# Expert biases as three float32r matmuls, and w_down's rows in contiguous groups, in a mixture-of-experts block

## The chip, the cores and the metric

The kernel runs on one core of a Trainium2 chip. The metric is the device time of one execution in microseconds (us). Names used here: PE is TensorE, PEld its weight loads, DVE VectorE, ACT ScalarE, POOL GpSimd, SP SyncE, which here does nothing but issue DMAs. L77 is line 77 of the kernel before.

## The reference

One layer of a diffusion backbone, for 256 latent tokens and 256 context tokens of 1024 numbers, all float32. A first half mixes tokens (a modulated norm, an input projection, a state-space scan and a gated delta net beside each other, an output projection, a residual). The second half, in which the change lies, is a mixture of 32 experts, of which each token uses 4:

```python
logits = t @ w_router + b_router
top_val, top_idx = lax.top_k(logits, 4)
weights = softmax(top_val)                      # -> combine[token, expert]
for e in range(32):
    gu = t @ w_gate_up[e] + b_gate_up[e]        # 1024 -> 2048
    gate, up = gu[:, :1024], gu[:, 1024:]
    gate = minimum(gate, 7.0); up = clip(up, -7.0, 7.0)
    act = (up + 1.0) * gate * sigmoid(gate * 1.702)
    out = out + combine[:, e:e+1] * (act @ w_down[e] + b_down[e])
x = rmsnorm(x + gt2 * out, norm_f)
```

## The kernel before

**Stages.** `front()` is the first half of the layer and ends with `merge()` (the output projection and the second norm); `moe()` is the router and the experts. All engines but SP get their order from a scheduler that goes by priorities in program order; SP's order is that in which the code issues its loads.

**An expert.** Its tokens are gathered into 64 slots (`gather`: products with one-hot matrices `oh`). Class `Expert` then computes in four steps. `gu(end)` multiplies the slots' columns `xT` (128 rows x 64 slots, stationary) by row chunks of w_gate_up, 128 rows of 2048 columns each; there are 8. The two halves of the array's columns work side by side: gate and up are tiles of 512 columns in PSUM, of which one half of 1024 hidden columns lies on partitions 0 to 63 and the other on 64 to 127. `swiglu` makes `ut` of them, `down` transposes `ut` to `aT` and multiplies by w_down in 4 pieces of 256 rows, `weigh` and `scatter` add the result to the tokens. In `moe()` the steps of two experts interleave:

```python
cur.gu(6); nxt = expert(e + 1); cur.gu(8); cur.swiglu()
nxt.gu(4); cur.down(); nxt.gu(5); cur.weigh(); cur.scatter()
```

**Weights.** An expert takes 12 tiles `w` of 1 MiB, 8 of w_gate_up and 4 of w_down: 384 in all, 8 matmul instructions each in the trace. `moe_stream` gives their order, `wload` issues them on SP's queue into a ring of 18 buffers (`WREG`), which the front's tensors leave in that order; 10 loads go ahead of the experts. Twelve buffers are of 8 KB per partition. The others (K, four of `ld`, `s1`) are two tiles of 4 KB, so that a weight tile comes in two DMAs of 512 KB, with runs of 4 KB per partition. A w_down tile puts rows 256f + p and 256f + 128 + p on partition p: two runs of 4 KB, in any buffer.

**Biases.** `bias` holds b_gate_up as 128 rows of 512 (four for each expert) and b_down as 64 rows. A product adds one row to all slots: its stationary matrix is a column of the identity, broadcast over 64 columns (`row`), its moving one `bias`. There are 4 such float32 products ahead of an expert's first w_gate_up chunk and 2 ahead of its first w_down chunk, 12 instructions in the trace, as `bias,ident`. Below b_down lie two rows of norm_f, which two products and two ACT copies spread over the partitions for the last expert.

## Time and profile before

| | |
|---|---|
| Time, 3 runs | 1507.41 us median, 1506.1 to 1511.52 |
| Span of the profiled execution | 1498.9 us |
| Front | 0 to some 501 us |
| Last output projection and routing | 501 to 532 us |
| Experts | 532 to 1484 us |
| End (scatter, last norm, output) | 1484 to 1498.9 us |

The profiled execution has no device time of its own beside the span; the runs' median is 8.5 us above it. The page gives busy times of the engines, the span in 40 slices, and what the DMA engines moved. A weight tile is 1.0486 MB, so bytes of the weights' queue and counted `w` matmuls can be set against each other stretch by stretch.

### The profile page before, as it was taken

Reading aid. Unit: us, or ns where it says so; the run is one execution under the profiler, and the core shown is the slowest. Engines: PE = TensorE matmul, PEld = TensorE weight load, DVE = VectorE, ACT = ScalarE, POOL = GpSimd, SP = SyncE. Lnnn points to the kernel's source line nnn. Section 1 sums busy time; section 2 is a strip of 40 time slices with the busy share of each in tenths; the row PEclk is TensorE's granted clock in tenths of the full one; section 3 lists DMA queues with packets and bytes.
Section 4 is the critical chain, followed back from the end, with each engine's and each line's share of the span. In section 5 each row is a group of like instructions: output and inputs, shape, how many; then the busy total and the mean of one; then the engine's idle time right before and its main releaser. Section 6 shows DMA issues by size and latency. Waiting matters only on the chain. (4 is left out here: it accounts for less than half of the span.)

```text
span 1498.9 us, 20035 instructions
## 1 busy us (share of the span) xinstructions
PE 1407.0 (94%) x8102; PEld 659.2 (44%) x8102; DVE 556.6 (37%) x1070; ACT 263.7 (18%) x578; POOL 203.2 (14%) x272
## 2 busy tenths in 40 slices
PE   5798796799989999999999999999999999999995
PEld 2275474687667543333333333333333333333331
DVE  3878788554424421232213212321321222123123
ACT  3434233233300111010101101110111111011111
POOL 1728499321100000000000000000000000000000
PEclk9699898799989999999999999999999999999997
DMA  9465355831185889999999999999999999999993
GB/s 309 133 192 118 130 166 145 134 93 43 48 266 185 307 320 368 415 415 413 414 414 415 413 415 415 414 415 412 415 414 416 415 411 416 413 416 411 413 414 147
DMA packets 157259, 473.22 MB, mean 316 GB/s; under 512 B 29090, under 2 KB 68175, under 8 KB 135081
## 3 DMA queue, kind: packets, MB, share of 16 engines
q1 hardware_dynamic: 137501, 460.06, 79.6%
q10 hardware_dynamic: 19276, 10.77, 3.3%
q0 software_dynamic: 384, 1.05, 0.6%
q8 instruction: 66, 1.08, 0.3%
q14 instruction: 32, 0.26, 0.0%
HBM read 467.68 MB, written 4.15 MB: 315 GB/s over the span
## 5 line engine op out<-in xcount | busy, mean ns | idle before, releaser
L77 PE MATMUL ps<-w,xT 128*64 128x512 f32 x2048 | 485.0, 598 | 0.1
L77 PEld LDWEIGHTS ps<-w,xT 128*64 128x64 f32 x2048 | 141.9, 137 | 279.9 <-issue 251.5
L77 PE MATMUL ps<-w,aT 128*64 128x512 f32 x1024 | 233.3, 599 | 0.7 <-ACT aT L83 0.7
L1701 DVE SCALAR_TENSOR_TENSOR od<-ps,cs,gt 128x512 f32<-128x512 f32 x32 | 24.0, 751 | 494.1 <-PE ps L77 494.1
L77 PEld LDWEIGHTS ps<-w,aT 128*64 128x64 f32 x1024 | 76.7, 138 | 146.9 <-issue 137.4
L80 POOL TENSOR_TENSOR frs<-frs,mhalf 128x1 f32<-128x1 f32 x2 | 1.1, 540 | 970.9 <-DVE frs L340 970.9
L77 PE MATMUL ps<-h,wsp 128*128 128x256 f32 (+1 forms) x672 | 113.2, 317 | 17.2 <-ACT gs L83 6.7
L80 DVE TENSOR_TENSOR x<-x,ps 128x512 f32<-128x512 f32 x128 | 85.2, 684 | 86.5 <-PE ps L77 86.5
L77 PEld LDWEIGHTS ps<-h,wsp 128*128 128x128 f32 x672 | 94.7, 202 | 35.5 <-issue 9.6
L77 PE MATMUL ps<-bias,ident 128*64 128x512 f32 (+2 forms) x388 | 101.4, 605 | 0.1
L83 ACT ACTIVATE odh<-od 128x512 fp32r<-128x512 f32 x31 | 19.5, 629 | 419.8 <-DVE od L1701 419.8
L80 DVE TENSOR_TENSOR wsp<-win,wsp 128x512 fp32r<-128x512 f32 x72 | 60.9, 852 | 41.0 <-ACT wsp L83 40.6
L77 PE MATMUL ps<-hh,wsp 128*128 128x512 f32 x192 | 55.9, 422 | 15.1 <-DVE wsp L80 13.4
L77 PE MATMUL ps<-h,oh 128*64 128x512 f32 x248 | 63.8, 602 | 0.0
L77 PE MATMUL ps<-wm,sc 128*32 128x512 f32 x192 | 48.5, 671 | 14.5 <-DMA wm<-in_w_mod_dram 14.5
L83 ACT ACTIVATE wsp<-win 128x512 fp32r<-128x512 f32 x72 | 43.7, 626 | 70.9 <-PE ps L77 28.1
L83 ACT ACTIVATE aT<-ps 128x512 f32<-128x512 f32 x32 | 19.1, 597 | 181.3 <-PE ps L1686 181.3
L77 PEld LDWEIGHTS ps<-bias,ident 128*64 128x64 f32 (+2 forms) x388 | 23.0, 134 | 62.4 <-issue 29.1
L83 ACT ACTIVATE sgm<-gt 128x512 f32<-128x512 f32 x32 | 20.1, 628 | 170.1 <-DVE gt L1673 170.1
L77 PEld LDWEIGHTS ps<-hh,wsp 128*128 128x128 f32 x192 | 36.1, 198 | 30.3 <-DVE wsp L80 15.4
L703 DVE SCALAR_TENSOR_TENSOR cacc<-raw,cols,cacc 128x512 f32<-128x512 f32 (+1 forms) x48 | 46.0, 959 | 5.9 <-ACT cacc L83 5.5
L1673 DVE TENSOR_SCALAR gt<-ps 128x512 f32<-128x512 f32 x32 | 22.1, 691 | 55.1 <-PE ps L77 55.1
(369 smaller groups left out, 1464.4 us busy)
## 6 DMA issues: line engine op xcount, KB each, us to landing
w<-in_w_gate_up_dram SPq DMA_DIRECT2D x172, 1024.0 KB
w<-in_w_gate_up_dram SPq DMA_DIRECT2D x168, 512.0 KB
w<-in_w_down_dram SPq DMA_DIRECT2D x84, 1024.0 KB
w<-in_w_down_dram SPq DMA_DIRECT2D x88, 512.0 KB
wm<-in_w_mod_dram SPq DMA_DIRECT2D x48, 512.0 KB
win<-in_w_in_dram SPq DMA_DIRECT2D x36, 512.0 KB
wo<-in_w_out_dram SPq DMA_DIRECT2D x8, 512.0 KB
wa<-in_w_branch_a_dram SPq DMA_DIRECT2D x4, 512.0 KB
```

The source lines that it names most:

```text
L77: self.nc.tensor.matmul(out, lhsT, rhs, start=start, stop=stop, **kw)
L80: (eng or self.nc.vector).tensor_tensor(out, a, b, op=op)
L83: self.nc.scalar.activation(out, in_, func, **kw)
L703: nc.vector.scalar_tensor_tensor(acc[:, rows], rt[:, rows, k:k + 64], sc, acc[:, rows], op0=OP.mult, op1=OP.add)
L1673: V.tensor_scalar(gt, pz[0], 7.0, None, op0=OP.min)
L1701: V.scalar_tensor_tensor(od, self.pd, self.cs, k.gt2, op0=OP.mult, op1=OP.mult)
```

## The change

- **Biases.** A product in float32r takes one pass, but does not keep all bits of a float32, so the biases are split into two parts that each fit and add up exactly. `bias` becomes three tiles of 128 rows: the upper parts of 64 bias rows on partitions 0 to 63, the remainders on 64 to 127. Each is loaded twice (`braw`, two DMAs of 128 KB on ACT's queue, in a buffer of `s5`), copied by ACT into float32r, and DVE subtracts the copy on the lower half. `dup` is a 64-column matrix with two ones in each column. For each expert two POOL copies (`pick`) broadcast its columns into stationary tiles `selsg` (for gate and up) and `selsd` (for down), one buffer each. Two products of 128x128 on 512 columns add the gate and up biases, one the down bias.
- **w_down.** Partition p of a half of w_down now gets four rows in sequence, 4p to 4p + 3; a tile takes two of them, one run of 8 KB. The transposes of `ut` read every fourth column to match.
- **The buffer K** is one tile of 8 KB per partition, so its weight tiles come in one DMA.
- **norm_f** is broadcast by a DMA on GpSimd's queue into the buffer R3, in place of two products and two copies.
- **Other buffers.** gt2 moves from tag g1 to rw; `mod2`'s bias row is loaded at its step (4, 1), in a buffer of `s5`. The overflow path, which runs only where an expert has more than 64 tokens, changes in the same way.

The diff, without comments and docstrings:

```diff
-    TAGS = dict(s1=(1024, 2), s5=(512, 4), p5=(512, 3), g1=(1024, 2), g5=(512, 3), c2=(256, 4), rw=(544, 2), cs=(4, 3))
-    REGS = ("H0", "H1", "R0", "R1", "R2", "R3", "U", "XC", "XL", "V", "Q", "PA", "PB", "GA")
+    TAGS = dict(s1=(1024, 2), s5=(512, 4), p5=(512, 3), g1=(1024, 2), g5=(512, 3), c2=(256, 4), rw=(544, 2), cs=(4, 3),
+                sg=(256, 1), sd=(128, 1))
+    REGS = ("H0", "H1", "R0", "R1", "R2", "R3", "U", "XC", "XL", "V", "Q", "PA", "PB", "GA", "K")
...
-    def rr(self, reg, name):
-        assert reg == "K"
-        return [self.wk.tile([128, 1024], F32, name=name, tag=f"r{reg}{i}", bufs=1) for i in range(2)]
...
+                    ps.append(self.pt("o"))
+                if (j, b) == ((0, 0) if nb == 1 else (4, 1)):
...
-                    ps.extend([self.pt("o"), bm])
-                p, bm = ps
+                    ps.append(bm)
+                p, bm = ps[0], ps[-1]
...
-        return self.mod_run(2048, 2, None)
+        return self.mod_run(2048, 2, "s5")
...
-        self.ct = self.rr("K", "ct")
+        self.ct = self.r("K", "ct").rearrange("p (a d) -> p a d", a=2)
...
-            nc.sync.dma_start(self.ct[a], dram(I["ctx"], 128 * D * a, [[D, 128], [1, D]]))
+            nc.sync.dma_start(self.ct[:, a], dram(I["ctx"], 128 * D * a, [[D, 128], [1, D]]))
...
-        src = [ct[0], ct[1], self.xt[:, 0], self.xt[:, 1]]
+        src = [ct[:, 0], ct[:, 1], self.xt[:, 0], self.xt[:, 1]]
...
-                self.kT = [t[:, x:x + 512] for t in self.rr("K", "kT") for x in (0, 512)]
+                k = self.r("K", "kT")
+                self.kT = [k[:, 512 * i:512 * i + 512] for i in range(4)]
...
-        dn = lambda e, f: dram(I["w_down"], (e * D + f * 256) * D, [[D, 128], [128 * D, 2], [1, D]])
+        dn = lambda e, f: dram(I["w_down"], (e * D + 512 * (f // 2) + 2 * (f % 2)) * D, [[4 * D, 128], [1, 2 * D]])
...
-        if rg == "K":
-            return self.rr(rg, "w")
...
-                    self.nc.sync.dma_start(w[0][:, f * D:f * D + D], src[:, f])
+                    self.nc.sync.dma_start(w[0][:, f * D:f * D + D], src[:, f * D:f * D + D])
...
-        bias = self.w([128, 2, 512], "bias", "g1")
-        for i, (nm, a, b) in enumerate((("b_gate_up", 0, 128), ("b_down", 0, 64), ("norm_f", 64, 66))):
-            nc.scalar.dma_start(bias[a:b, min(i, 1)], dram(I[nm], 0, [[512, b - a], [1, 512]]))
-        self.gt2 = self.w([128, 512], "gt2", "g1")
+        bt = [self.w([128, n], nm, "g1", F32R) for n, nm in ((1024, "bias"), (576, "biad"))]
+        bias = [bt[0][:, :512], bt[0][:, 512:], bt[1][:, :512]]
+        for i, (nm, r) in enumerate((("b_gate_up", 0), ("b_gate_up", 64), ("b_down", 0))):
+            t = self.w([128, 512], "braw", "s5")
+            for h in range(2):
+                nc.scalar.dma_start(t[64 * h:64 * h + 64], dram(I[nm], 512 * r, [[512, 64], [1, 512]]))
+            self.act(bias[i], t, AF.Copy)
+            self.tt(bias[i][64:], t[64:], bias[i][64:].bitcast(F32), OP.subtract)
+        dup = bt[1][:, 512:]
+        self.tt(dup, self.ident[:, :64], self.ident[:, 64:], OP.add)
+        self.gt2 = self.w([128, 512], "gt2", "rw")
...
-        row = lambda n, x: self.ident[:n, x:x + 1].to_broadcast([n, CAP])
+        def pick(x, n, tag):
+            v = self.w([128, n * CAP], "sel" + tag, tag, F32R)
+            nc.gpsimd.tensor_copy(v.rearrange("p (n s) -> p n s", s=CAP), dup[:, x:x + n, None].to_broadcast([128, n, CAP]))
+            return v
...
-                for h in range(2):
-                    p = self.pt("s")
-                    self.mm(p, self.ident[64:66, 64 + h:65 + h].to_broadcast([2, 128]), bias[64:66, 1], start=True, stop=True)
-                    self.act(self.nf[:, 512 * h:512 * h + 512], p, AF.Copy)
+                nc.gpsimd.dma_start(self.nf[:, :D], dram(I["norm_f"], 0, [[0, 128], [1, D]]))
+            sg, sd = pick(4 * e % 64, 4, "sg"), pick(2 * e, 2, "sd")
...
-                       lambda q: (row(128, 4 * e + q), bias[:, 0]), lambda q: (row(64, 2 * e + q), bias[:64, 1]))
+                       lambda i: (sg[:, 128 * i:128 * i + 128], bias[e // 16]), (sd, bias[2]))
...
-                self.overflow(pos, cmb, cnt, io64, row)
+                self.overflow(pos, cmb, cnt, io64)
...
-    def overflow(self, pos, cmb, cnt, io64, row):
+    def overflow(self, pos, cmb, cnt, io64):
...
-            pc = self.w([128, NE, 4], "pc", "rw")
+            pc = self.w([128, NE, 4], "pc", "c2")
...
+            row = self.w([4, 4 * CAP], "row", "c2")
+            V.tensor_copy(row.rearrange("p (n s) -> p n s", s=CAP), self.ident[:4, :4, None].to_broadcast([4, 4, CAP]))
...
-                        pe = self.w([128, 4], "pe", "rw")
+                        pe = self.w([128, 4], "pe", "c2")
...
-                        wd = I["w_down"][0, bass.ds(e, 1)].rearrange("o (f p) d -> (o p) f d", p=128)
-                        x = Expert(self, lambda j: self.wload(wg[:, j]), lambda f: self.wload(wd[:, 2 * f:2 * f + 2]),
-                                   lambda q: (row(4, q), brow), lambda q: (row(2, q), drow))
+                        wd = I["w_down"][0, bass.ds(e, 1)].rearrange("o (h p r) d -> (o p) h r d", p=128, r=4)
+                        x = Expert(self, lambda j: self.wload(wg[:, j]), lambda f: self.wload(wd[:, f // 2, 2 * (f % 2):2 * (f % 2) + 2]),
+                                   lambda i: (row[:, 128 * i:128 * i + 128], brow), (row[:2, :128], drow))
...
-    """one expert on up to CAP tokens; the two column halves of the array hold the two halves of
-    the hidden (then of the model) dimension"""
...
-            for q in range(4):
-                k.mm(self.pz[q // 2][self.HALF[q % 2]], *self.bgu(q), start=True, stop=False)
+            for i in range(2):
+                k.mm(self.pz[i], *self.bgu(i), start=True, stop=False)
...
-        for dh, r in enumerate(self.HALF):
-            k.mm(pd[r], *self.bdn(dh), start=True, stop=False)
+        k.mm(pd, *self.bdn, start=True, stop=False)
...
-        for q in range(4):
-            k.nc.tensor.transpose(pa[:, 128 * q:128 * q + 128], self.ut[:, 128 * q:128 * q + 128], k.ident)
+        uv = self.ut.rearrange("p (c r) -> p r c", r=4)
+        for r in range(4):
+            k.nc.tensor.transpose(pa[:, 128 * r:128 * r + 128], uv[:, r], k.ident)
...
-                f = 2 * fb + f2
-                hf, q = f // 4, f % 4
+                hf, x = fb // 2, 2 * (fb % 2) + f2
...
-                    k.mm(pd[r], aT[:, q, 64 * hf:64 * hf + 64], w(2 * f2 + dh), start=False, stop=(f == 7))
+                    k.mm(pd[r], aT[:, x, 64 * hf:64 * hf + 64], w(2 * f2 + dh), start=False, stop=(fb == 3 and f2 == 1))
```

The next rows are in the programs' own order, not timed. First PE in the middle of the experts, before the change: from the fifth `w,xT` chunk of an expert to its last w_down tile (`bias,ident` the biases, `ident,ut` the transposes, `h,oh` the next expert's gathering).

```order
L77 MATMUL ps<-w,xT 64x512 x4
L77 MATMUL ps<-bias,ident 64x512 x2
L77 MATMUL ps<-w,xT 64x512 x4
L77 MATMUL ps<-bias,ident 64x512 x2
L77 MATMUL ps<-w,xT 64x512 x4
L77 MATMUL ps<-bias,ident 64x512 x2
L1686 MATMUL ps<-ident,ut_6912 128x128 x4
L77 MATMUL ps<-h_4343,oh 64x512 x4
L77 MATMUL ps<-w,xT 64x512 x12
L77 MATMUL ps<-w,aT 64x512 x16
```

The same place with the change:

```order
L73 MATMUL ps<-w,xT 64x512 x4
L73 MATMUL ps<-biad,selsd 128x512
L73 MATMUL ps<-w,xT 64x512 x4
L73 MATMUL ps<-bias,selsg 128x512 x2
L73 MATMUL ps<-w,xT 64x512 x4
L1696 MATMUL ps<-ident,ut_6621 128x128 x4
L73 MATMUL ps<-h_4339,oh 64x512 x4
L73 MATMUL ps<-w,xT 64x512 x12
L73 MATMUL ps<-w,aT 64x512 x16
```

Three pairs of float32 products give way to one float32r product ahead of w_down (`biad,selsd`) and two for the next expert's gate and up (`bias,selsg`); each stands between products of `w`.

SP in one round of the ring, before the change. 128x2048 is a tile in one DMA, 128x2x1024 one in one DMA with two runs per partition, 128x1024 one half of a tile in two.

```order
L1422 DMA w<-in_w_gate_up_dram 128x2048 x5
L1422 DMA w<-in_w_down_dram 128x2x1024 x4
L1422 DMA w<-in_w_gate_up_dram 128x2048
L1425 DMA w<-in_w_gate_up_dram 128x1024 x8
L1422 DMA w<-in_w_gate_up_dram 128x2048
L1425 DMA w<-in_w_gate_up_dram 128x1024 x2
L1422 DMA w<-in_w_gate_up_dram 128x2048
L1425 DMA w<-in_w_down_dram 128x1024 x2
L1422 DMA w<-in_w_down_dram 128x2x1024 x3
```

The same with the change:

```order
L1420 DMA w<-in_w_gate_up_dram 128x2048 x7
L1420 DMA w<-in_w_down_dram 128x2048 x4
L1420 DMA w<-in_w_gate_up_dram 128x2048
L1423 DMA w<-in_w_gate_up_dram 128x1024 x8
L1420 DMA w<-in_w_gate_up_dram 128x2048
L1423 DMA w<-in_w_gate_up_dram 128x1024 x2
L1420 DMA w<-in_w_gate_up_dram 128x2048
L1420 DMA w<-in_w_down_dram 128x2048 x4
L1420 DMA w<-in_w_gate_up_dram 128x2048 x7
```

The two-run loads have become 128x2048, and the two halves in the buffer K one load; the loads of two halves in `ld` and `s1` stay.

ACT in the routing, before the change, from the first squares of the second norm (`junk`) to the first columns of the first expert (`xT`; `x1T` are the router's inputs, `small` is the softmax):

```order
L83 ACTIVATE junk_4346,ss_4344<-x_4342 128x512
L280 DMA xt_4320<-in_x_dram 64x1024 x2
L83 ACTIVATE junk_4346,ss_4344<-x_4342 128x512
L83 ACTIVATE x1T<-ps 128x4x128
L83 ACTIVATE junk_4346,ss_4344<-x_4342 128x512
L83 ACTIVATE x1T<-ps 128x4x128
L83 ACTIVATE junk_4346,ss_4344<-x_4342 128x512
L83 ACTIVATE x1T<-ps 128x4x128 x2
L83 ACTIVATE small<-small 128x8
L83 ACTIVATE xT<-ps 128x64
```

The same with the change, where `braw` are the raw biases:

```order
L79 ACTIVATE bias<-braw 128x512
L1454 DMA braw<-in_b_gate_up_dram 64x512 x2
L79 ACTIVATE x1T<-ps 128x4x128
L1454 DMA braw<-in_b_down_dram 64x512
L79 ACTIVATE x1T<-ps 128x4x128
L79 ACTIVATE junk_4342,ss_4340<-x_4338 128x512
L1454 DMA braw<-in_b_down_dram 64x512
L79 ACTIVATE x1T<-ps 128x4x128 x2
L79 ACTIVATE bias<-braw 128x512
L79 ACTIVATE small<-small 128x8
L79 ACTIVATE biad<-braw 128x512
L79 ACTIVATE xT<-ps 128x64
```

Three copies of the biases and four of their six loads now stand between these rows; the first two loads stand just ahead of them.

## Rows read from the trace of the kernel before

**Rows 1.** The page: busy time by engine, GB/s in 40 slices.
```profile
PE 1407.0 (94%) x8102; PEld 659.2 (44%) x8102; DVE 556.6 (37%) x1070; ACT 263.7 (18%) x578; POOL 203.2 (14%) x272
...
GB/s 309 133 192 118 130 166 145 134 93 43 48 266 185 307 320 368 415 415 413 414 414 415 413 415 415 414 415 412 415 414 416 415 411 416 413 416 411 413 414 147
```

**Rows 2.** Busy time of the tile `w` alone, by stretch (columns in the first line).
```profile
core 0: us, PE busy (x) PEld busy (x), PEclk, DMA share, GB/s
600.00:1440.00 840.00, 621.21 (x2724) 192.08 (x2721) 1.00 1.02 414
1440.00:1458.00 18.00, 15.45 (x70) 4.90 (x72) 1.00 1.03 412
1458.00:1484.00 26.00, 18.03 (x68) 4.96 (x64) 0.87 0.56 225
```

**Rows 3.** Queue of the weights in the same stretches: packets, MB, share of 16 engines.
```profile
q1 hardware_dynamic: 72560, 347.34, 101.8%
...
q1 hardware_dynamic: 1833, 7.39, 102.4%
...
q1 hardware_dynamic: 1412, 5.76, 55.2%
```

**Rows 4.** Packets by size: 599.5 to 616.8, 617 to 629.5, 600 to 1440 us.
```profile
DMA packets 1020, 7.27 MB, mean 420 GB/s; under 512 B 109, under 2 KB 109, under 8 KB 156
...
DMA packets 1370, 5.12 MB, mean 409 GB/s; under 512 B 137, under 2 KB 137, under 8 KB 1356
...
DMA packets 72602, 347.93 MB, mean 414 GB/s; under 512 B 7038, under 2 KB 7038, under 8 KB 53288
```

**Rows 5.** Timeline of one expert, PE, then its weight loads (PEld).
```profile
917.71 1.03 PE L77 MATMUL ps<-bias,ident 128*64 128x512 f32 x4
...
918.67 0.66 PE L1686 MATMUL ps<-ident,ut 128*128 128x128 f32 x4
...
917.72 0.14 PEld L77 LDWEIGHTS ps<-bias,ident 128*64 128x64 f32 x2 [0.29 <-issue]
...
918.67 0.42 PEld L1686 LDWEIGHTS ps<-ident,ut 128*128 128x128 f32 x4 [0.81 <-issue]
```

**Rows 6.** Timeline of PE in the input projection, float32r matmuls.
```profile
144.27 1.08 PE L77 MATMUL ps<-h,wsp 128*128 128x512 f32 x4
145.19 1.07 PE L77 MATMUL ps<-hh,wsp 128*128 128x512 f32 x4
```

**Rows 7.** Busy time of each engine by stretch; PE, PEld, DVE, ACT, POOL, PEclk, DMA share, GB/s.
```profile
0.00:501.00 501.00, 426.86 (x3567) 307.75 (x3568) 305.21 (x604) 148.07 (x330) 199.78 (x267) 0.91 0.55 155
100.00:150.00 50.00, 43.34 (x419) 29.62 (x418) 36.28 (x31) 19.79 (x61) 34.88 (x22) 0.93 0.57 143
530.00:535.00 5.00, 5.00 (x19) 2.93 (x19) 0.53 (x3) 0.50 (x2) 0.00 (x0) 0.57 0.15 61
535.00:600.00 65.00, 64.87 (x314) 25.29 (x314) 10.48 (x21) 8.25 (x18) 0.00 (x0) 1.00 0.95 359
```

**Rows 8.** What SP waited for, 532 to 600 us: us, times, longest.
```profile
SPq L1422 <- PE ps L77: 29.8, 15, 6.2
SPq L1425 <- PE ps L77: 19.6, 12, 8.0
```

**Rows 9.** Timeline of the routing, 486 to 532 us.
```profile
486.07 0.82 ACTq L258 DMA_DIRECT2D n<-in_norm_dram  x2
...
498.17 0.69 DVE L259 SCALAR_TENSOR_TENSOR a<-a,n 128x512 f32<-128x512 f32 x1 [2.41 <-DMA n<-in_norm_dram]
...
519.64 2.80 PE L77 MATMUL ps<-bias,ident 128*64 128x512 f32 x12
...
526.73 0.21 ACT L83 ACTIVATE small<-small 128x8 f32<-128x8 f32 x1 [2.19 <-DVE small L80]
...
531.10 0.22 ACT L83 ACTIVATE xT<-ps 128x64 f32<-128x64 f32 x1 [4.16 <-PE ps L77]
```

**Rows 10.** Timeline of PE at the end.
```profile
1473.80 10.06 PE L77 MATMUL ps<-w,aT 128*64 128x512 f32 x32 [0.75 <-ACT aT L83]
```

## Prediction

> **What bounds the kernel now.** I read the page first: the busy times and the line of moved bytes [rows 1]. TensorE is busy in 94% of 1498.9 us, which looks like the bound; but from the 17th of the 40 slices on (600 us) the transfers stand at 411 to 416 GB/s without a dip, so in the stage of the experts two resources are full at once. Which of them ends last is a matter of lead, and that can be counted. A weight tile of 1 MiB is 8 matmul instructions in the trace. By the stretches of the tile `w` [rows 2], TensorE works off 2724 / 8 = 340.5 tiles between 600 and 1440 us, then 8.75, then 8.5. By the bytes of the weights' queue [rows 3], 347.34 / 1.0486 = 331.2 tiles land in the first stretch, 7.0 in the second and 5.5 in the third. Summed from the end, TensorE has 357.75 tiles still to do at 600 us and the transfers 343.7 still to bring: a lead of 14 tiles. At 1440 us it is 17.25 - 12.5 = 4.7 and at 1458 us 8.5 - 5.5 = 3.0, of which one is at work or half landed, so two whole ones lie ready. TensorE is never short of weights, but it is faster than the stream (840 x 12 / 340.5 = 29.6 us per expert against 840 x 12 / 331.2 = 30.4), lives off the lead, and comes to the end with almost none left. So a faster TensorE alone is worth about the lead; after that the stream is the bound, and only what speeds the stream counts.
>
> **The biases on TensorE.** Removed: per expert 12 instructions of `bias,ident`. Four take from 917.71 to 918.67 [rows 5], so 0.24 us each and 2.9 us in all, the turn of the array behind them included. Added: three float32r matmuls 128x128 on 512 columns. Rows of this shape and type stand in the front: four from 144.27 to 145.19, 0.23 us each [rows 6]: 0.7 us. They need the array in one piece while `w` runs in column halves, so each of the two places has a turn in and out: four turns. The nearest row is the turn from the halves to the transposes at 918.67: a matmul of `w` takes 621.21 / 2724 = 0.228 us [rows 2], and TensorE starts there 0.05 us after four of these. But the weight loads of the same place are idle for 0.81 us where 0.29 is usual [rows 5]: a turn costs 0.05 us if the matmuls already queued cover the late load, and 0.52 if none do, as could be with one or two short matmuls between two turns. I take 0.1, near the row of the matmuls themselves. Gain per expert: 2.9 - 0.7 - 4 x 0.1 = **1.8 us**, with bounds of 2.2 (turns for nothing) and 0.1.
>
> **What TensorE's gain is worth.** 32 x 1.8 = 58 us would pass the stream long before the end. To pay the whole gain below it has to save 10 / 32 = 0.3 us per expert. So what it gives directly is the lead at the end. The tile that starts at 1458 us had lain there for one load (2.5 us) and a little: **3 us**, with bounds of 0 (the chain behind the last tile absorbs it) and 5 (both ready tiles).
>
> **The stream.** Two edits lengthen runs from 4 to 8 KB per partition: w_down's rows in contiguous pairs, and the buffer K in one piece. The rows of packets [rows 4] price it: between 599.5 and 616.8 us 864 of 1020 packets are of 8 KB, and 420 GB/s flow; between 617 and 629.5 us nearly all are of 4 KB, and it is 409 GB/s. A tile takes 2.497 and 2.564 us: 0.067 us between them. Between 600 and 1440 us (53288 - 7038) / 256 = 181 tiles come in 4 KB runs and 19314 / 128 = 151 in 8 KB runs: 54.5% short. Mixed so, the two prices give 2.533 us, what the 414 GB/s of that stretch say, so they are consistent. Of the 18 buffers of the ring 5 stay in two pieces, 28%. Of 344 tiles 0.267 x 344 = 92 change: 92 x 0.067 = **6.2 us**. Bounds: 0, if what separates the two windows is not the length of a run, and 9, since the slices of the page scatter by 5 GB/s [rows 1] and the 11 between the windows could be 16.
>
> The Trainium skill's page "DMA: Bandwidth & Descriptors" (section "Why small descriptors are slow (HBM only)") puts a fixed cost of about 3 cycles on each packet, beside one beat per 32 bytes. By that, a 4 KB packet spends 131 cycles where 8 KB spend 259: 1.1% per tile, an estimate of 2.6 us in all where the rows give 6.2. Both have one sign; the sum goes by the rows.
>
> **What the stream has to carry more.** norm_f comes as a broadcast of 0.52 MB into a buffer of the ring; on a full stream that is 0.52 / 414 GB/s = **1.3 us** lost (0 if it lands in a gap). The biases are 0.77 MB instead of 0.39, before the experts: at most **0.9 us** lost, nothing where the stream idles.
>
> **The start of the stage.** From 530 to 600 us the stream isn't full: 61 GB/s for 5 us and 359 for 65 [rows 7], 4.3 and 8.6 us worth of bytes at 414. There SP waits for TensorE to give buffers back, 49 us in that stretch [rows 8]. TensorE finishes over two experts by 600 us, so it gives buffers back up to 2 x 1.8 = 3.6 us earlier, and what isn't lost there stays: **3 us** gained, with bounds of 0 and 8.6.
>
> **Front and routing.** Before the routing 12 of the old matmuls take 2.80 us [rows 9], in a place where TensorE waits for nothing; fewer of the new ones stand there, and half of the 2 us may reach the routing: **1 us** gained, bounds of 0 and 2.1. `mod2`'s bias row and gt2 move to other buffers, and the scheduler puts many front instructions in another order. No row prices that; TensorE is idle for 74 of the front's 501 us [rows 7], and I let a reordering shift a fifteenth of it: +-5 us, taken as nothing. The split itself (three ACT copies, three DVE subtractions) is a rival, below. The 64 POOL copies go to an engine that is busy for 0.00 us from 535 to 600 [rows 7]; each is wanted an expert after its predecessor, 30 us, so it costs nothing unless it takes that long. Strided columns read by the transposes, 38 loads less on SP's queue: SP waits for buffers and landings there, nothing else is queued on it, so nothing.
>
> **The clock.** TensorE will wait some 2 us per expert (30.2 - 27.8), a busy share of 92%. In the front, 100 to 150 us has a share of 87% and a granted clock of 0.93, while the unbroken stretch from 535 to 600 us has 1.00 [rows 7]. While it waits anyway a slower clock costs little; what counts are the matmuls after the last landing, 10.06 us long before [rows 10]. I take **1 us** lost.
>
> **Sum.** 3 + 6.2 + 3 + 1 - 1.3 - 0.9 - 1 = 10.0 us; span 1488.9. The median of the runs, 1507.41, is 8.5 us over the profiled span, which I take as what lies around it: 1497.4, say 1497 us. From no change I can tell 0.5% of the time, 7.5 us: faster is under 1499.9, slower over 1514.9.
>
> **Rivals.**
> (a) *The longer runs bring nothing*: the two windows differ by something else (they also differ in which matrix is read). Then 1497.4 + 6.2 = 1503.6, within 0.5%. For it speaks that the windows are short; against it, that the mix predicts the long stretch's rate. 0.13.
> (b) *The clock*: a TensorE that waits for each tile falls to the lower level, 1.2 GHz. If it then fell behind it would stop waiting, so it can't lose more than the end: the last 32 matmuls take 10.06 us [rows 10] where 32 x 0.228 = 7.3 would be full speed, so 0.73 of it; wholly at half they take 14.6, and the 16 gate and up matmuls ahead of them 3.6 more. 1502 to 1506. Against it: waits of 0.2 us per tile, and clocks of 0.9 at similar shares. 0.13. The Trainium skill's page "TensorE: Matmul & The Clock Gate" (section "HAM oscillation — how this bites in real kernels") tells of a kernel whose clock falls at each wait for a DMA; no row here shows it with waits this short.
> (c) *The turns of the array eat the gain*: from (2.9 - 0.7 - 0.3) / 4 = 0.48 us per turn on, TensorE stays the bound and the time stays at 1505 to 1508. 0.05. The Trainium skill's page "TensorEngine Tiling (Array Packing)" (section "Key Properties") says that a change of tiling mode drains the engine, without a price.
> (d) *The other side: the routing waits for the split biases.* The six loads sit in ACT's queue in three pairs, each ahead of the ACT copy and the x1T or softmax work of the routing, and the loads of the second pair stand behind the copy that waits for the first. The norm's loads took 12.1 us from that queue (issued 486.07, used 498.17 [rows 9]). By ACT's order the first pair goes out after the second norm's first squares, which I put at about 505 us (an estimate, 19 us behind the norm's loads); three pairs one after the other land at 541.5; the copy into biad stands ahead of the first xT, which came at 531.10: everything behind, weights' buffers too, is 11 us late, and the 4 us gained at start and routing are gone: 1512. It decides from 10 us of delay on; under (531.1 - 505) / 3 = 8.7 us a pair nothing is late. 0.11, of which half above 1514.9 with an unlucky reordering.
>
> **Chances.** The forecast has 0.58. Its own range, 1490 to 1502, comes from the bounds (lead 0 to 5, runs 3 to 9, start 0 to 7). Up to (a) to (d), with no more than 2 in 10 outside: 1487 to 1508. Faster: nearly all of the forecast and a little of (b): 0.62. Same: (a), (c), most of (b), part of (d): 0.29. Slower: part of (d) and a bad reordering: 0.09.
>
> **What would show it.** Right: in the stage of the experts the busy share of TensorE falls from 100% to about 93%, with short waits on `w` named by DMA, at 417 GB/s; the groups `bias` cost under 1 us per expert; loads of 8 KB runs give 72% of the tiles; the tail of 16 us is unchanged. Wrong: a TensorE still at 100% (c); a rate still at 414 (a); clocks far below 0.9 after 600 us (b); the first `xT` of the experts later than 531.10, with ACT or DVE waiting for `braw` (d).

## The result: slower by 1%

The changed kernel takes 1522.66 us (median; 1520.19 to 1529.87) beside 1509.47 of the kernel before: a ratio of 1.0102, interval 1.0069 to 1.0136. I had forecast 1497, and 1508 was the end of the range. The profiled execution has a span of 1518.5 us. It lies 4.2 us under the median given here and that of the kernel before 10.6 under its own, so of the 19.6 us between the two spans 13.2 show in the medians.

The page, as in [rows 1] (L73 is line 73 of the changed kernel):

```profile
PE 1380.1 (91%) x7810; PEld 663.1 (44%) x7810; DVE 558.5 (37%) x1074; ACT 265.5 (17%) x579; POOL 226.7 (15%) x337
...
GB/s 306 136 192 108 143 163 146 129 56 43 70 101 177 316 244 353 414 417 416 417 417 418 420 417 418 417 417 418 420 418 416 417 416 417 419 419 417 415 417 207
```

The stream rose to 414 to 420 GB/s, as forecast, and TensorE's share fell from 94 to 91%; but the stream is full only from the 17th slice of a longer span on, and in the 12th it stands at 101 GB/s where [rows 1] have 266. The time went ahead of the experts. Stage by stage, from the starts of matmuls in the timelines of both profiled executions:

| | before | after | |
|---|---|---|---|
| first `Yt,A` to last `M,Yt` | 12.0 | 27.9 | +15.9 |
| last `M,Yt` to first `yaT,wa` | 92.8 | 105.5 | +12.7 |
| first to last `yaT,wa` | 40.7 | 44.4 | +3.7 |
| last `wo,gs` to first `w,xT` (routing) | 14.9 | 19.9 | +5.0 |
| first `w,xT` at | 532.3 | 563.7 | +31.4 |
| first `w,xT` to last `w,aT` (experts) | 951.0 | 939.3 | -11.7 |

The rows ahead of the experts add up to 31.4 us with two that the table leaves out: the first `Yt,A` starts 4.4 us earlier, and the stretch from the last `yaT,wa` to the last `wo,gs` is 1.6 us shorter.

**The experts did about what the sum said**: 11.7 us less in this execution, where its terms for the stage (3 + 6.2 + 3 - 1.3 - 1) give 9.9. Busy time of `w` by stretch, as in [rows 2]; then packets and the weights' queue in the second of these stretches, as in [rows 4] and [rows 3]; then what PE waited for, and its busy time from 1000 to 1400 us (columns as in [rows 7]):

```profile
632.00:832.00 200.00, 156.43 (x680) 47.98 (x678) 1.00 1.02 417
632.00:1472.00 840.00, 636.28 (x2758) 184.57 (x2754) 1.00 1.02 417
```

```profile
DMA packets 61577, 350.68 MB, mean 417 GB/s; under 512 B 6828, under 2 KB 6828, under 8 KB 30778
...
q1 hardware_dynamic: 61444, 349.72, 101.3%
```

```profile
PE ps L73 <- DMA w<-in_w_down_dram: 22.1, 33, 1.5
PE ps L73 <- DMA w<-in_w_gate_up_dram: 7.1, 12, 0.9
```

```profile
1000.00:1400.00 400.00, 375.60 (x1710) 127.81 (x1710) 98.22 (x176) 44.45 (x94) 10.90 (x26) 1.00 1.02 418
```

While weights lie ready TensorE takes 200 x 12 / 85 = 28.2 us per expert, forecast 27.8. Over the long stretch the stream brings 349.72 / 1.0486 = 333.5 tiles in 840 us, 30.2 us per expert, forecast 30.2; (30778 - 6828) / 256 = 94 of them come in 4 KB runs, 28% as the ring has it. Now TensorE waits for weights, 45 times and 1.5 us at most, and is busy for 94% of the time at a granted clock of 1.00; in the kernel before no wait of this stage is put down to a weight's DMA. The biases of one expert, as in [rows 5]:

```profile
1096.07 0.50 PE L73 MATMUL ps<-biad,selsd 128*128 128x512 f32 x1
1096.50 1.94 PE L73 MATMUL ps<-w,xT 128*64 128x512 f32 x8
1098.46 0.47 PE L73 MATMUL ps<-bias,selsg 128*128 128x512 f32 x1
1099.23 0.51 PE L73 MATMUL ps<-bias,selsg 128*128 128x512 f32 x1 [0.29 <-DVE ut L1685]
1099.66 1.94 PE L73 MATMUL ps<-w,xT 128*64 128x512 f32 x8
1101.53 0.75 PE L1696 MATMUL ps<-ident,ut 128*128 128x128 f32 x4
```

One float32r matmul between two groups of `w` takes 0.43 us until the next starts, two take 1.2 us, of which 0.29 wait for `ut`. And the end, as in [rows 10]: 7.09 us at a granted clock of 1.00, where it had been 10.06 at 0.69 on average.

```profile
1496.45 7.09 PE L73 MATMUL ps<-w,aT 128*64 128x512 f32 x32 [0.75 <-ACT aT L79]
```

**The front lost 26 us, the routing 5.** The state-space half's 32x32 matmuls (`Yt,A`, `M,Yb`, `M,Yt`, from the line of `gdn_b`) stand between columns of the input projection (`h,wsp`, 128x128), which the scheduler puts where it likes. Before, on PE:

```profile
309.37 7.46 PE L77 MATMUL ps<-h,wsp 128*128 128x256 f32 x57
...
316.77 1.09 PE L77 MATMUL ps<-Yt,A 32*32 32x32 f32 x29
...
320.63 2.17 PE L77 MATMUL ps<-h,wsp 128*128 128x256 f32 x16
...
322.73 2.21 PE L77 MATMUL ps<-M,Yb 32*32 32x32 f32 x64
...
324.86 1.93 PE L77 MATMUL ps<-h,wsp 128*128 128x256 f32 x14
```

After:

```profile
305.61 2.53 PE L73 MATMUL ps<-h,wsp 128*128 128x256 f32 x19
...
312.44 1.27 PE L73 MATMUL ps<-Yt,A 32*32 32x32 f32 x29 [4.31 <-DVE Yt L1107]
...
324.39 0.58 PE L73 MATMUL ps<-h,wsp 128*128 128x256 f32 x1
...
324.90 0.31 PE L73 MATMUL ps<-M,Yb 32*32 32x32 f32 x2
...
325.14 0.58 PE L73 MATMUL ps<-h,wsp 128*128 128x256 f32 x1
...
325.65 0.31 PE L73 MATMUL ps<-M,Yb 32*32 32x32 f32 x2
```

Before, 57 `h,wsp` cover the time until `Yt` is there, and the kinds follow each other in blocks: 0.13 us for an `h,wsp`, 0.03 for an `M,Yb`. After, 19 are left for that place, TensorE waits 4.31 us, and then single `h,wsp` alternate with pairs of 32x32 matmuls at 0.75 us a pair of places. Busy times and granted clock of the same 20 us, before and then after (columns as in [rows 7]):

```profile
320.00:340.00 20.00, 20.00 (x273) 17.67 (x270) 10.31 (x15) 8.95 (x17) 3.74 (x4) 1.00 0.19 54
```

```profile
320.00:340.00 20.00, 20.00 (x160) 15.45 (x159) 4.85 (x6) 4.36 (x8) 3.73 (x4) 0.50 0.10 27
```

TensorE is busy in 100% of both, at a granted clock of 1.00 and of 0.50, the lower of its two levels. Some of the 12.7 us in the second line of the table are moved work: 262 `h,wsp` stand in that stretch instead of 226. In the third line TensorE waits for the loads of `wa`, 11.4 us instead of 6.8. The program's order, known ahead of the run, shows the places of single `h,wsp`. Its rows on PE after the change, where the kernel before has blocks of 16:

```
L73 MATMUL ps<-Yb,A 32x32 x10
L73 MATMUL ps<-h_120,wsp 128x256
L73 MATMUL ps<-Yb,A 32x32
L73 MATMUL ps<-h_120,wsp 128x256
L73 MATMUL ps<-Yb,A 32x32
```

The routing, first ACT and then PE, to be read beside [rows 9]:

```profile
538.30 1.16 ACTq L1454 DMA_DIRECT2D braw<-in_b_gate_up_dram  x2
...
544.65 0.63 ACT L79 ACTIVATE bias<-braw 128x512 fp32r<-128x512 f32 x1 [4.38 <-DMA braw<-in_b_gate_up_dram]
...
546.04 1.12 ACTq L1454 DMA_DIRECT2D braw<-in_b_gate_up_dram  x2
...
547.21 0.60 ACT L79 ACTIVATE x1T<-ps 128x512 f32<-128x512 f32 x1 [1.92 <-PE ps L73]
...
546.15 0.70 PE L73 MATMUL ps<-bias,selsg 128*128 128x512 f32 x2 [0.88 <-DVE bias L76]
...
547.86 1.18 PE L73 MATMUL ps<-wra,x1T 128*128 128x32 f32 x8 [1.00 <-ACT x1T L79]
...
563.66 2.96 PE L73 MATMUL ps<-w,xT 128*64 128x512 f32 x8
```

ACT stands 4.38 us at the copy that waits for the first raw biases; its x1T is behind it and behind the issue of the next two loads, and on PE the router's `wra,x1T` waits for that behind the first bias products.

### The profile page after: what moved, and what is told of

It is laid out like the page before. It is cut to its first block, busy times and chain, and to the rows that moved or that the text cites. A ratio compares the mean times of both kernels' runs of the same rounds, so it can differ in the third digit from the quotient of the medians.

```text
span 1518.5 us, 19575 instructions
## 1 busy us (share of the span) xinstructions
PE 1380.1 (91%) x7810; PEld 663.1 (44%) x7810; DVE 558.5 (37%) x1074; ACT 265.5 (17%) x579; POOL 226.7 (15%) x337
## 5 line engine op out<-in xcount | busy, mean ns | idle before, releaser
L73 PE MATMUL ps<-w,xT 128*64 128x512 f32 x2048 | 484.5, 600 | 7.2 <-DMA w<-in_w_gate_up_dram 7.1
L73 PE MATMUL ps<-w,aT 128*64 128x512 f32 x1024 | 235.4, 597 | 23.7 <-DMA w<-in_w_down_dram 22.1
L73 PEld LDWEIGHTS ps<-w,xT 128*64 128x64 f32 x2048 | 137.6, 137 | 270.4 <-issue 238.6
L73 PEld LDWEIGHTS ps<-w,aT 128*64 128x64 f32 x1024 | 69.9, 136 | 182.3 <-issue 116.5
L73 PE MATMUL ps<-h,wsp 128*128 128x256 f32 (+1 forms) x672 | 123.7, 332 | 11.4 <-DVE wsp L76 5.1
L1506 POOL CAST selsd<-biad 128x128 fp32r<-128x128 f32 x32 | 9.4, 294 | 717.1 <-PE ps L73 717.1
L73 PEld LDWEIGHTS ps<-h,wsp 128*128 128x128 f32 x672 | 101.0, 212 | 29.5 <-issue 10.2
L73 PE MATMUL ps<-h,oh 128*64 128x512 f32 x248 | 63.0, 604 | 0.0
L73 PE MATMUL ps<-hh,wsp 128*128 128x512 f32 x192 | 56.0, 421 | 7.4 <-DVE wsp L76 4.6
L73 PE MATMUL ps<-wm,sc 128*32 128x512 f32 x192 | 45.8, 668 | 15.2 <-DMA wm<-in_w_mod_dram 15.2
L73 PEld LDWEIGHTS ps<-hh,wsp 128*128 128x128 f32 x192 | 35.9, 197 | 23.1 <-DVE wsp L76 6.6
L1506 POOL CAST selsg<-biad 128x256 fp32r<-128x256 f32 x32 | 16.9, 529 | 179.5 <-PE ps L73 173.2
L73 PEld LDWEIGHTS ps<-odh,ST 64*128 64x128 f32 x124 | 12.0, 183 | 52.2 <-issue 16.2
```

What stands on the lines that cost most here:

```text
L73: self.nc.tensor.matmul(out, lhsT, rhs, start=start, stop=stop, **kw)
L1506: nc.gpsimd.tensor_copy(v.rearrange("p (n s) -> p n s", s=CAP), dup[:, x:x + n, None].to_broadcast([128, n, CAP]))
```

## The experiments

The ratio is to the kernel before on the same chip; stages as in the table above, each from the one profiled execution, so they carry that execution's clock. The wait is TensorE's ahead of the first `Yt,A`, the clock the mean granted one from there to the last `M,Yt` (the kernel before: no wait, 1.00; the changed one: 4.3 us, 0.51).

| | median us | ratio, interval | wait, clock | `Yt,A` to `M,Yt` | routing | experts at | long |
|---|---|---|---|---|---|---|---|
| e1_front_moves | 1530.58 | 1.0150 (1.0111 to 1.0189) | 5.0, 0.50 | 28.3 | 16.5 | 566.7 | 951.5 |
| e2_gt2_late | 1508.41 | 1.0018 (0.9992 to 1.0044) | 6.1, 0.50 | 20.3 | 19.7 | 554.2 | 945.2 |
| e3_mod_row_only | 1512.34 | 1.0038 (1.0006 to 1.0070) | 4.7, 0.69 | 16.1 | 15.3 | 549.3 | 948.1 |
| e4_gt2_only | 1501.09 | 0.9965 (0.9940 to 0.9990) | none, 1.00 | 12.7 | 17.0 | 535.0 | 947.9 |
| e5_front_kept | 1501.30 | 0.9958 (0.9928 to 0.9988) | none, 0.87 | 13.5 | 18.7 | 537.8 | 941.9 |
| e6_front_kept_bias | 1505.51 | 0.9992 (0.9964 to 1.0020) | none, 1.00 | 11.9 | 19.3 | 537.9 | 949.0 |
| e7_stream_only | 1506.58 | 0.9994 (0.9963 to 1.0025) | none, 0.57 | 18.6 | 14.9 | 548.0 | 948.9 |
| e8_no_alternation | 1508.54 | 1.0024 (0.9995 to 1.0052) | 4.3, 0.52 | 19.8 | 19.6 | 549.5 | 941.8 |
| e9_early_biases | 1521.13 | 1.0105 (1.0058 to 1.0151) | 5.2, 0.50 | 28.3 | 13.5 | 557.7 | 944.0 |
| e10_kept_early | 1494.27 | 0.9919 (0.9886 to 0.9952) | none, 0.57 | 18.5 | 13.3 | 539.0 | 943.6 |
| e11_gate_later | 1507.00 | 1.0003 (0.9973 to 1.0032) | 5.0, 0.68 | 21.5 | 20.4 | 545.5 | 941.5 |
| e12_two_words | 1503.08 | 0.9986 (0.9958 to 1.0013) | 5.1, 0.70 | 15.8 | 13.8 | 541.5 | 941.8 |

In all eight profiled executions with this wait (the changed kernel's is one) the clock fell to 0.50 during it or within 1 us behind it. Of the six without, the kernel before, e4 and e6 stayed at 1.00; e5, e7 and e10 fell 2.7 to 3.8 us behind the first `Yt,A`.

**e1: the two moves of buffers alone, on the kernel before.**

```diff
-        return self.mod_run(2048, 2, None)
+        return self.mod_run(2048, 2, "s5")        # and modrow at step (4, 1)
-        self.gt2 = self.w([128, 512], "gt2", "g1")
+        self.gt2 = self.w([128, 512], "gt2", "rw")
-            pc = self.w([128, NE, 4], "pc", "rw")  # pe likewise
+            pc = self.w([128, NE, 4], "pc", "c2")
```

> The kernel before, with nothing of the change but the two moves of buffers in the front: mod2's bias row in a buffer of s5 from step (4, 1) on, and gt2 in rw (with pc and pe in c2). The biases, w_down, K and norm_f are as before. Theory 1 (the moves alone make the scheduler order the front otherwise, and that costs what the changed kernel lost): the experts begin 25 to 31 us later than in the kernel before, from 557 to 563 us, with the single h,wsp matmuls between pairs of 32x32 ones again; the experts last as long as before or, with the ring fuller at their start, up to 5 us less; 1530 to 1540 us. Theory 2 (the new bias path or its buffers make the front late): as before, 1505 to 1513 us, experts from about 532 us.

24 us slower, with the alternation and 28.3 us in its place, and experts as long as before; they begin 4 us past the range. Theory 1: two moves that the prediction priced at nothing cost 24 us; what the changed kernel does besides gives 8 of them back.

**e2: gt2 late, on the changed kernel.**

```diff
-... for n, nm in ((1024, "bias"), (576, "biad"))]
+... for n, nm in ((1024, "bias"), (1024, "biad"))]
-        dup = bt[1][:, 512:]
+        dup = self.con.tile([128, 64], F32R, name="dup")
-        self.gt2 = self.w([128, 512], "gt2", "rw")
+        self.gt2 = bt[1][:, 512:].bitcast(F32)
```

> The changed kernel, with gt2 not in rw but beside b_down's biases in the tile biad of g1, so that its load can't be issued early in the front; dup has a tile of its own. All else of the change stays, mod2's bias row in s5 too. Theory 1: the front's order has no single h,wsp between 32x32 matmuls, the experts begin at 528 to 540 us, and the gain in the experts (12 us in the changed kernel; less where the ring is less full at their start, 8 to 12) shows: 1495 to 1506 us. Theory 2: still 1515 to 1523 us. If the routing waits for the biases (the prediction's case d), the experts begin 5 to 11 us later than the end of the output projection would let them.

14 us better than the changed kernel, without the alternation (20.3 us), but the experts begin at 554, not 540, and 1508.41 us is over the range: only half of what theory 1 wanted. The wait ahead of `Yt,A` is still there, with 24 `h,wsp` for cover, and the routing still takes 19.7.

**e3 and e4: each move alone, on the kernel before** (the lines of e1, parted).

> The kernel before, with mod2's bias row alone moved (s5, from step (4, 1) on). Theory 1 in its form that it takes both moves: the experts begin within 6 us of the kernel before, 1502 to 1516 us. If this move alone is the cause: 1525 to 1540 us.

> The kernel before, with gt2 alone moved to rw (pc and pe to c2). Theory 1 in its form that it takes both moves: the experts begin within 6 us of the kernel before, 1502 to 1516 us. If this move alone is the cause: 1525 to 1540 us.

mod2's row alone costs 0.4%, gt2 alone gains 0.35%; neither has the alternation, and both together cost 1.5%. e3 does have the wait ahead of `Yt,A`, and its experts begin 17 us later than before, not within 6; e4 has neither, and its time is 1 us under the range. So the moves don't add up: what they do is to turn the scheduler's order, and the order has the price.

**e5 and e6: the front's order put back; e6 without the longer runs.** Beside the lines of e2 for `bias` and gt2:

```diff
-                if (j, b) == ((0, 0) if nb == 1 else (4, 1)):      # modrow early again
-        return self.mod_run(2048, 2, "s5")
+        return self.mod_run(2048, 2, None)
+        selb = self.w([128, 448], "selb", "rw", F32R)              # selsg, selsd, dup
-        self.tt(dup, self.ident[:, :64], self.ident[:, 64:], OP.add)
+        V.scalar_tensor_tensor(dup, self.ident[:, :64], one, ...)  # one = (braw == braw)
```

> The changed kernel with the front's order put back: mod2's bias row has its own buffer and its early step again, gt2 shares the tile biad of g1, and the matrices selsg, selsd and dup lie in one tile of rw, dup written after the first biases have landed. By the program's order PE has 58 h,wsp matmuls to do ahead of Yt,A (57 in the kernel before, 19 in the changed one) and no run of single ones between 32x32 matmuls. Theory 1 (the front's order is what was lost, the experts' part of the change gains as forecast): no wait over 1 us ahead of Yt,A, a granted clock of 1.00 from 300 to 340 us, experts from 528 to 538 us and 6 to 12 us shorter than 951; 1494 to 1502 us beside 1506 of the kernel before. Rival (the gain in the experts was only there because they began late, with a full ring): experts 949 to 952 us long and 1504 to 1510 us.

> The kernel of e5_front_kept without the longer runs: w_down's rows and the two halves of the buffer K as in the kernel before. The biases, norm_f and the buffers are those of e5. By the prediction's sum the longer runs are worth 6 us of the stream once TensorE has the faster biases: the experts 5 to 7 us longer than in e5, time 5 to 7 us over e5; if TensorE were still the bound, the same as e5.

In both, `selsd` already holds the next expert's columns when the down product reads it, so they add the next expert's b_down: the same instructions on other numbers. e5 is 0.4% faster than the kernel before, its experts 941.9 us long; e6 is level with it, 949.0. The experts' gain thus doesn't hang on their late start, the rival of e5. The clock in e5's 32x32 place, expected to be 1.00, was 0.87. So with the biases in place the longer runs are worth 7.1 us by the stages and 4.2 by the medians, where the sum had 6.2. Experts begin at 538 in both, 5.5 later than before, 4 of them in the routing.

**e7: the longer runs alone, on the kernel before** (`dn`, the columns of `ut`, K in one tile).

> The kernel before with the longer runs alone: w_down's rows in contiguous groups and K in one tile. PE's order is that of the kernel before up to the experts. If TensorE sets the end before the change (the prediction's reading of the lead), a faster stream alone brings nothing: experts 949 to 952 us, 1504 to 1508 us, with a lead at the end that is some 6 us larger. If the stream was the bound already: 6 us faster, 1499 to 1502 us.

No gain. The stream rises to 417 GB/s while TensorE stays busy in all of 600 to 1440 us (last row):

```profile
301.00:321.00 20.00, 19.91 (x383) 17.56 (x376) 13.76 (x34) 5.07 (x10) 6.11 (x8) 1.00 0.58 131
320.00:340.00 20.00, 20.00 (x264) 19.36 (x260) 5.75 (x8) 6.57 (x12) 4.41 (x5) 0.54 0.16 44
600.00:1440.00 840.00, 840.00 (x3920) 297.30 (x3918) 205.04 (x366) 93.26 (x197) 0.00 (x0) 1.00 1.02 417
```

TensorE was the bound, as the lead had said. The first two rows tell something too: PE's order here is that of the kernel before, and yet this execution ran 320 to 340 us at 0.54 and took 18.6 us for the 32x32 place, and the experts began at 548. So the clock there differs between executions of one order, and with it the stages of the table; over the last 29 runs of the kernel before the mean granted clock went from 0.954 to 0.967 and the time from 1497.64 to 1516.05.

**e8 and e11: the alternation taken away by one number of the front's order**, on the changed kernel. `ORDER` names the steps of the front (`br` and `gate` belong to its branches); the number behind @ is an offset of the step's priority.

```diff
e8
-        ... s5_out br@60 gate@300 br@1500 br@60 br@1500*3 gdn_b br@1500
+        ... s5_out br@60 gate@300 br@1500 br@1500 br@1500*3 gdn_b br@1500
e11
+        ... s5_out br@60 gate@1500 br@1500 br@60 br@1500*3 gdn_b br@1500
```

> The changed kernel with one number of the front's order changed: one of the steps br comes with priority offset 1500 in place of 60. By the program's order this takes away the 17 places at which a single h,wsp matmul (128x128) stands between 32x32 matmuls, and leaves the 19 h,wsp ahead of Yt,A, so the wait there stays. If the turns of the array cost there what their rows suggest (some 0.35 us a place at a halved clock): 6 to 9 us between Yt,A and M,Yt saved, 1513 to 1518 us. If the time is the clock's alone, which falls at the wait: no more than 2 us, 1519 to 1524 us.

> The changed kernel with another single number of the front's order changed than in e8: one of the steps gate comes with priority offset 1500 in place of 300. By the program's order this too takes away the single h,wsp matmuls between 32x32 ones and leaves 19 h,wsp ahead of Yt,A. If it is these places that cost the time, and not something else that e8's number moved: as e8, 1504 to 1514 us, with Yt,A to M,Yt 18 to 21 us. If e8's gain came from elsewhere: 1516 to 1525 us.

Both are 14 to 16 us faster than the changed kernel by the medians, 12 to 15 by the ratios; of e8 I had expected 6 to 9, from this place alone. On PE in e8:

```profile
315.57 1.23 PE L73 MATMUL ps<-Yt,A 32*32 32x32 f32 x29 [4.34 <-DVE Yt L1107]
...
321.45 3.78 PE L73 MATMUL ps<-h,wsp 128*128 128x256 f32 x16
...
325.16 3.62 PE L73 MATMUL ps<-M,Yb 32*32 32x32 f32 x64
```

The wait is there and the clock is at half, as in the changed kernel; the blocks take 0.23 us for an `h,wsp` and 0.055 for an `M,Yb`. At that clock one `h,wsp` and two 32x32 matmuls would be 0.34 us, in the alternation they take 0.75: 0.41 us for a turn of the array and back (with the weight loads that it may hold up), 17 times, 7 us; 27.9 against 19.8, at a clock of 0.51 and 0.52, is 8.1. The rest of what e8 and e11 gave back lies behind this place (in both the span from the first to the last `yaT,wa` is 36 us, not 44). The two numbers move other steps as well, so that rest isn't tied to the alternation.

**e9: the raw biases in other buffers**, on the changed kernel.

```diff
-            t = self.w([128, 512], "braw", "s5")
+            t = self.w([128, 512], "braw", "g5")
```

> The changed kernel with the raw biases in buffers of g5 in place of s5, one word. By the program's order the four loads of b_gate_up go out ahead of the third junk, and all three ACT copies stand ahead of the x1T of the routing. In every kernel with split biases so far the time from the last wo,gs to the first w,xT was 19 us, in those without 15 to 16. If ACT and the matmuls behind it wait there for the loads (the mechanism of the prediction's case d): 15 to 16 us here too, and 3 to 5 us less time than the changed kernel, 1517 to 1520 us. If the longer routing has another cause (the float32r matmuls, the copies themselves): still 19, and the time of the changed kernel, 1520 to 1525 us.

ACT, then PE:

```profile
529.82 2.05 ACTq L1454 DMA_DIRECT2D braw<-in_b_gate_up_dram  x3
...
536.91 1.27 ACT L79 ACTIVATE bias<-braw 128x512 fp32r<-128x512 f32 x2 [3.54 <-DMA braw<-in_b_gate_up_dram]
...
545.46 0.71 PE L73 MATMUL ps<-bias,selsg 128*128 128x512 f32 x2
...
546.13 1.08 PE L73 MATMUL ps<-wra,x1T 128*128 128x32 f32 x8
...
557.74 3.68 PE L73 MATMUL ps<-w,xT 128*64 128x512 f32 x8
```

The loads leave 8.5 us earlier, the copies are done ahead of x1T, and the routing takes 13.5 us, 6.4 less than in the changed kernel and 1.4 less than before. The stage went as the theory says, the time did not: in this execution the experts take 4.7 us longer (944.0), the median of 1521.13 lies in the range of the rival, and the ratio is that of the changed kernel. Six runs leave open whether anything was gained; e12 tests it again.

**e10 and e12: parts together.** e10 is e5 with e9's word; e12 is the changed kernel with e8's number and e9's word.

```diff
e10
-            sg, sd = pick(4 * e % 64, 4, "sg"), pick(2 * e, 2, "sd")
+            sg = pick(4 * e % 64, 4, "sg")         # sd is picked in down()
```

> The kernel of e5_front_kept with the raw biases in g5 as in e9, and selsd filled when the down product is emitted, so that it holds this expert's columns (in e5 and e6 it held those of the next expert, so that b_down of the next one was added: the same work on other numbers). All three theories of the parts together: front as in the kernel before, routing 15 to 16 us, experts 941 to 943 us as in e5. Experts from 530 to 535 us, 1493 to 1499 us; if the parts don't add up (the stream, which then starts later against the experts, takes it back): 1499 to 1503 us.

> The changed kernel with the two small edits of e8 and e9 together (one br at 1500 in place of 60, the raw biases in g5). If they are separate causes they add up: 4 us under e8, 1502 to 1507 us, about the kernel before or a little under it. If the routing's delay is hidden behind something once the front is shorter: as e8, 1507 to 1510 us.

e12 is 5.5 us under e8, within the range, and e10 is 7 us under e5 with the same word: the routing's wait was on the path. Every profiled execution with `braw` in s5 has a routing of 18.7 to 20.4 us (six kernels), every one with it in g5 13.3 to 13.8 (three). e10 is 0.8% faster than the kernel before and 28 us faster than the changed one. Its experts began at 539, not by 535: its profiled execution ran the 32x32 place at a clock of 0.57. Its lowest run is 1487.63. It beats both kernels.

## Why the prediction was wrong

- **The step that failed** is in "Front and routing": "I let a reordering shift a fifteenth of it: +-5 us, taken as nothing". The term measured +24 us (e1), nearly five times its bound. I had bounded it by TensorE's idle time, as if an order could only move idle time about. In the row below (the changed kernel's front, beside the first of [rows 7]) TensorE is idle for 83 of 533 us, 9 more than the 74 of [rows 7]; 23 us more are busy time, of about as many matmuls. The order also sets how often the array turns (17 places, 7 to 8 us) and whether there is work to cover a wait (57 or 19 `h,wsp`), and in every execution with that wait the clock fell at it. The rows of the program's order that show both were known ahead of the run; I used them only at the places where the diff adds or removes instructions.

```profile
0.00:533.00 533.00, 450.16 (x3580) 327.01 (x3581) 307.96 (x610) 149.18 (x332) 196.31 (x267) 0.88 0.54 149
```

- **The routing** was a second miss in the same term: 1 us gained was forecast, 5 were lost (19.9 against 14.9). The mechanism is of the kind of case (d), a copy on ACT waiting for the split biases, but at another place. The first loads took 6.3 us, not 12.1, and by (d)'s own limit (8.7 us a pair) nothing would have been late; (d) priced the last copy, ahead of the first xT, where the wait that counts is at the first, with the router's x1T behind it. e12 and e10 show it in the time, e9 in the stage alone.
- **The biases on TensorE** were right but for the size of a turn: 28.2 us per expert where 27.8 was forecast, 1.4 us gained of 1.8, and 45 short waits on `w`. Less 0.23 us for each matmul, the rows above leave 0.20 us for two turns around one and 0.45 around two: 0.1 to 0.2 us each, against the 0.1 that I took. The strided columns, taken as nothing, make the weight load of a transpose longer, 210 ns for 140 (medians of 128), but the transpose itself only 284 for 273.
- **What they are worth, and the stream.** The longer runs alone bring nothing (e7). For the biases alone this is less clear: e6 is level, but its routing takes 4 us more than before, and its experts take 2.0 us less, near the lead's 3. Both parts together are faster (e5, e10). The stream's term (6.2) measured 4.2 to 7.1. The estimate worked out from the Trainium skill's page "DMA: Bandwidth & Descriptors" (section "Why small descriptors are slow (HBM only)") was 2.6; the measured numbers stand nearer to the rows' price.
- **The start of the stage** (3 us) came: over the 70 us that begin 2.7 us ahead of the first `w,xT`, the stream moves 338 GB/s before and 352 after (rows below), 1.0 MB or 2.4 us at 417 GB/s. And where the end was to lose 1 us to the clock, the last 32 matmuls took 3 us less, at a clock of 1.00.

```profile
529.60:599.60 70.00, 69.87 (x330) 28.51 (x331) 11.37 (x27) 8.76 (x20) 0.00 (x0) 0.97 0.89 338
561.00:631.00 70.00, 69.84 (x328) 28.97 (x330) 12.04 (x28) 8.76 (x20) 1.39 (x4) 0.97 0.91 352
```

- **The 8.5 us** that the sum adds to the span are not what lies around it. In every listed run the time is 1.6 to 2.3 us over its span; the rest is that execution's own, at a mean granted clock of 0.963. A gain counted from the median comes to the same forecast, but the stage times before carry that clock.
- **In sum**, with the front's order and the routing put back (e10), 1494.27 us was measured where the sum says 1497. That the totals agree is in part luck: the routing gained 1.6 us there where 1 was forecast, the experts 7.4 where 9.9 were, and its front ran at another clock. Rival (a) fell with e5 and e6, (c) with the 94% busy share, (b) with a granted clock of 1.00 from 566 us to the end of the stage.

What stays open: why the granted clock of the 32x32 stretch differs between executions of one order without a wait (1.00 in the kernel before, 0.57 in e7), and what the loss between 340 and 490 us comes from, beyond the moved `h,wsp` and the waits for `wa`. How much the wait ahead of `Yt,A` costs by itself wasn't measured: filling it with other work was not tried.

## What to carry to other kernels

Where a scheduler places the work, a change of a buffer's tag is a change of the whole program's order: compare the order of every engine from the first row on, not only around the edit, and price three things there: matmuls of other shapes one by one between each other, the work left to cover each wait, and what stands behind a copy that waits for a load. When two resources run nearly level, speeding one alone brings little (here nothing for the stream, some 2 us for TensorE); plan both edits and measure them together. And compare a stage over several executions before its length is put down to an edit: one order took 12.0 us and 18.6 us for the same place.

## What the runs showed that I had not expected

- A turn of the array between 128x128 and 32x32 matmuls and back cost 0.41 us at half clock (0.75 us for one and two matmuls that take 0.34 in blocks). The Trainium skill's page "TensorEngine Tiling (Array Packing)" (section "Key Properties") says that a change of mode drains the engine; the lost time agrees with it.
- The granted clock stood at 0.50 for 20 us in which TensorE was busy 100% of the time, on small matmuls and alternating ones, after one wait of 4.3 us; and in e7 it fell in the same place with no wait over 1 us from 296 us up to there (busy 19.91 of the 20 us ahead). The Trainium skill's page "TensorE: Matmul & The Clock Gate" (section "HAM oscillation — how this bites in real kernels") ties a falling clock to waits for a DMA; e7's rows show a fall without one at that place.
